# Output projection from scaled float16 pairs, gate sums from bfloat16 trees

## The chip, the cores and the metric

The kernel runs on one core of a Trainium2 chip. A core has TensorE (PE in the profile, with its weight loads as PEld), VectorE (DVE), ScalarE (ACT), GpSimd (POOL) and SyncE (SP, which only issues DMAs). Each engine takes its instructions in the order in which the program gives them. The metric is device time in microseconds of one execution; a lower time is better.

## The reference

One layer of a bidirectional encoder over 1024 tokens of width 1024, in float32. All inputs of the two attention groups come from one projection, and all outputs go through one more:

```python
h = jnp.einsum('bsd,de->bse', x, w_in[layer])
q_a, k_a, v_a, z_a, q_b, k_b, v_b, z_b = jnp.split(h, SPLIT_POINTS, axis=-1)
y_a = neighborhood_attention(...)          # 8 heads, windows of 8 x 16 on a 16 x 64 grid, learned bias
y_b = windowed_gqa_with_sink(...)          # 8 heads on 2 key heads, |i - j| <= 128, rotary, sink logit
mixed = jnp.concatenate([y_a * jax.nn.silu(z_a), y_b * jax.nn.silu(z_b)], axis=-1)
y = jnp.einsum('bse,ed->bsd', mixed, w_out[layer])
x = layer_norm(DEEPNORM_ALPHA * x + y, ln_gain[layer], ln_bias[layer])
```

The change concerns the last matrix product, `mixed @ w_out`: `mixed` has 1024 rows and 1024 columns, `w_out` is 1024 by 1024, and ALPHA is the fourth root of 2.

## The kernel before, in words

**Precision by pairs.** A float32 operand is split into a high part in a shorter type and a low part that holds the rest, and a product is three matmuls: high by high, high by low, low by high. The input projections (`project`, L355) use float16 pairs, for which x and the weights are first brought to a known magnitude by powers of two. The output projection (`out_mms`, L899) uses float32r pairs of `mixed` (tiles `m`, in `mh` and `ml`) and of `w_out` (tiles `wo`, in `wo_parts`), without a scale.

**Stages.** First V is projected (L430), while x is loaded and split. Then comes a prologue of six projections of 48 matmuls each (`ORDER[:6]`: zb0, z0, zb1, kb, qb0, z1). A program count runs along with these 288 matmuls: `run_to` emits one matmul, adds one to `ran`, and then runs what `at(c, ...)` has put at that count. So `at(219, w_scale, NPRO)` stands in every engine's order where the 219th matmul stands in PE's. After the prologue come 128 units of attention, one per step: scores on PE (`stage_qk`, L709 and L710) into one of four banks of PSUM with tag "s", bias and row minimum on DVE (L719), exponential on ACT (`stage_exp`, L735), high part on ACT (L745), low part on DVE (L746, which is the last reader of the bank), a DMA transpose, and six to nine steps later the product with V (`stage_pv`, L774), normalisation and transposition (L783, L794). The output of a head pair is multiplied into its gate tile (`stage_ot`, L797 and L803), which then holds the columns of `mixed`.

**Fill.** Between the units PE works off the other fifteen projections and the first 60 matmuls of the output projection (`out_head`), in portions that `FILL_AT` fixes by step. Each projection writes into one of two banks with tag "pj". A bank is free again when its last reader is done; for the gate z1 these are a tanh on ACT (L318) and a multiply on DVE (L319).

**Order.** The prologue and the units are in the order of the program text. In the units, ACT, DVE, POOL and SP also have software queues: `enq` puts an operation in, `pop` emits one or two ready ones per step, lower `prio` first and older first among equals, and `need` emits what must come now. Only `final`, the last phase, is ordered by the scheduler of the framework, from the dependences and its own estimates of times. It splits the last four head pairs and weight tiles 8 to 15, does the remaining 348 matmuls of the output projection, adds the residual (L946), and normalises rows.

**Weight scales.** `w_scan` (L201) and `sum_w` (L595 on ACT, L597 on DVE) form row sums of absolute weights; `w_scale` adds them over the partitions by a matmul with ones (L207), reduces the result on DVE (L208) and rounds it to a power of two (L209 to L212). `v_scale` and `x_scale` do the like for V and x.

**Tiles of the output weights.** `wo_load` loads them as `WO_LD` gives the steps, `wo_split` splits them (high part L860 on ACT or DVE, low part L864 on DVE or POOL) at the steps of `WO_AT` or in `final`.

Of the kernel before, what the change touches and what calls it, by code (L numbers as in the profile page):

```python
# [15 lines left out]
S = 1024  # L16
# [15 lines left out]
NS = 21 - NPRO  # L32
NR = 8
# [9 lines left out]
M_AT = [105, 112, 118, 120]  # L43
WO_AT = [67, 71, 75, 79, 128, 129, 130, 131]
# [11 lines left out]
def hybrid_block(ctx, tc, xT, x, wt, wv, wo, bias, sink, gain, lbias, cos, sin, bmask, out):  # L56
# [52 lines left out]
    sg = const.tile([128, 3], F32, name="sg")  # L109
    rsg = const.tile([128, 1], F32, name="rsg")  # L110
# [88 lines left out]

    def w_scan(m):  # L200
        nc.scalar.activation(junk[:, :512], raws[m].rearrange("p k c -> p (k c)"), AF.Abs, accum_out=wm[:, m:m + 1])  # L201

    def w_scale(n):
# [3 lines left out]
        nc.tensor.matmul(ps[:, :m], ones, wm.bitcast(BF16)[:, 2 * c + 1:2 * (c + m):2], start=True, stop=True)  # L207
        nc.vector.tensor_reduce(g, ps[:, :m], axis=mybir.AxisListType.X, op=ALU.add if n < NPRO else ALU.max)  # L208
        nc.vector.tensor_scalar_max(g, g, 2.0 ** -30)  # L209
        nc.vector.tensor_scalar(g.bitcast(I32), g.bitcast(I32), 0x7F800000, None, op0=ALU.bitwise_and)  # L210
        nc.vector.tensor_scalar(wsc[:, n:n + 1].bitcast(I32), g.bitcast(I32), 0x7F800000, None, op0=ALU.bitwise_xor)
        nc.vector.tensor_scalar(v, g, xrs, 0.5, op0=ALU.mult, op1=ALU.mult)  # L212
# [111 lines left out]
    def z_col(e):  # L324
        return vsc if e in (4, 0, 5) else vscb[:, 0:1] if e == 1 else vscb[:, 1:2]
# [8 lines left out]
    def project(name):  # L334
        n = ORDER.index(name)
        w_split(2 * n + 2)
        for half in range(2):
            ps = new_group()
            for k in range(KT):
# [9 lines left out]
                if n + 2 < NPRO and half == 1 and k == 6:  # L349
                    w_scale(n + 2)  # L350
# [27 lines left out]


    ordered = ExitStack()  # L380
    with ExitStack() as vctx:
# [69 lines left out]
        def x_scale():  # L451
            ps = bank("t")
            nc.tensor.transpose(ps[:, :128], gm.to_broadcast([128, 128]), identf)
            nc.vector.tensor_reduce(gm, ps[:, :128], axis=AXX, op=ALU.max)
            nc.vector.tensor_scalar_max(gm, gm, 2.0 ** -16)
            nc.vector.tensor_scalar(gm.bitcast(I32), gm.bitcast(I32), 0x7F800000, None, op0=ALU.bitwise_and)
            nc.vector.tensor_scalar_mul(xrs, gm, 2.0 ** -14)
            nc.vector.reciprocal(xsc, xrs)
# [69 lines left out]
        for i in range(8):  # L528
# [6 lines left out]
            for k in range(KT):  # L535
                v_mms(ps, 4 + i // 2, i % 2, k)
                if i == 1 and k == 2:
                    x_scale()
                if i in (2, 3) and k == 4:
                    w_scale(i - 2)  # L540
# [12 lines left out]
        vg = vw.tile([128, 1], F32, name="vg")  # L553

        def v_scale():
# [4 lines left out]
            nc.vector.tensor_scalar_max(vg, vg, 2.0 ** -100)  # L560
            nc.vector.tensor_scalar(vg.bitcast(I32), vg.bitcast(I32), 0x7F800000, None, op0=ALU.bitwise_and)
            nc.vector.tensor_scalar_mul(vsc, vg, 2.0 ** -14)
# [25 lines left out]

        def sum_w(i):
# [4 lines left out]
            if i not in (1, 4, 7):  # L594
                nc.scalar.activation(junk[:, :1024], t, AF.Abs, accum_out=wm[:, c:c + 1])  # L595
            else:
                nc.vector.tensor_reduce(wm[:, c:c + 1], t, axis=AXX, op=ALU.add, apply_absolute_value=True)  # L597
# [4 lines left out]

        at(16, v_scale)
        for t in range(9):
# [3 lines left out]
        for i in range(NS):  # L608
            at(14 + 14 * i, sum_w, i)
# [211 lines left out]
    EO = (4, 5, 6, 7, 0, 1, 2, 3)  # L821

    def m_alloc(e, pool):
        for parts_ in (mh, ml):
            if pool is big:
                parts_[e] = big_tile(f"m{e}", (128, S))
            else:
                parts_[e] = pool.tile([128, S], F32R, tag="m", name=f"m{e}", bufs=8)

    def m_split(e, sl, hi, lo):  # L830
        hi(mh[e][:, sl], zt[e][:, sl])
        lo(ml[e][:, sl], zt[e][:, sl], mh[e][:, sl].bitcast(F32))

    WO_SEQ = [(e, a) for a in range(2) for e in EO[:4]] + [(e, a) for e in EO[4:] for a in range(2)]
    wo_parts = {}

    wo_raw = {}
# [12 lines left out]
    def wo_split(n):  # L850
        def hi():
            if n < 8:
                t = big_tile(f"wo{n}")
            elif n < 13:
                t = tiles["fp"].tile([128, 2, 512], F32R, tag="wo", name=f"wo{n}", bufs=5)
            else:
                t = zp.tile([128, 2, 512], F32R, tag=("zc", "zd", "ze")[n - 13], name=f"wo{n}", bufs=1)
            wo_parts[n] = [t[:, 0, :], t[:, 1, :]]
            copy = nc.scalar.copy if hi_eng == "act" else nc.vector.tensor_copy
            copy(wo_parts[n][0], wo_raw[n])  # L860

        def lo():
            h, l = wo_parts[n]
            eng.tensor_sub(l, wo_raw.pop(n), h.bitcast(F32))  # L864

        eng, q = (nc.vector, "dve") if n % 3 == 2 else (nc.gpsimd, "pool")
        hi_eng = "act" if clock["step"] is not None or WO_SEQ[n][1] == 1 else "dve"
        o = enq(hi_eng, hi, load_ops.get(("wo", n)))
# [7 lines left out]
    def m_queue(e):  # L876
        m_alloc(e, big)
        m_ops[e] = []
        for h in (slice(0, 512), slice(512, S)):
            o = enq("act", lambda h=h: nc.scalar.copy(mh[e][:, h], zt[e][:, h]))  # L880
            m_ops[e].append(enq("pool", lambda h=h: nc.gpsimd.tensor_sub(
                ml[e][:, h], zt[e][:, h], mh[e][:, h].bitcast(F32)), o))
# [33 lines left out]
    def final():  # L916
# [13 lines left out]
        gb, bb = gain_tile[0], zslot("bb")  # L930
        nc.sync.dma_start(bb, lbias.partition_broadcast(128))
# [7 lines left out]
        def residual(t, a, ps, c=None):  # L939
            if a == 0:  # L940
                stats[t] = fp.tile([128, 4, 6], F32, tag="stats", name="stats")
            for k in range(2) if t == 7 and c is None else (c,):
# [3 lines left out]
                nc.vector.scalar_tensor_tensor(xv, xv, ALPHA, ps[:, o:o + w], op0=ALU.mult, op1=ALU.add)  # L946
                nc.vector.bn_stats(stats[t][:, a if k is None else 2 * a + k, :], xv)

        def row_stats(t):
# [3 lines left out]
            nc.scalar.activation(sd, mv[:, 1:2], AF.Sqrt, bias=eps)  # L953
# [83 lines left out]
    clock["step"] = 0  # L1037
    for i in range(-LD, NU + LO):
# [9 lines left out]
        for n in range(len(WO_LD)):  # L1048
            if WO_LD[n] == i:
                load_ops["wo", n] = enq("sp", lambda n=n: wo_load(n), wo_ops.get({9: 0, 10: 1, 12: 2, 13: 3}.get(n)),  # L1050
                                        w_ops.get(17 + n if 4 <= n <= 8 else None))
        for n in range(len(WO_AT)):
# [26 lines left out]
        if 0 <= i - LT < NU:  # L1079
            stage_tr(units[i - LT])  # L1080
        pump_to(i + F1)
# [90 lines left out]
```

## Time and profile before

| | us |
|---|---|
| median of three runs (455.21 to 455.54) | 455.3 |
| the profiled execution's own time | 455.19 |
| its span, first to last instruction | 453.4 |
| PE busy | 443.6 |
| DVE busy | 333.3 |
| ACT busy | 287.7 |
| POOL busy | 227.7 |

The granted TensorE clock was 0.995 on average. The phases by the trace: V until 61.9 us, the prologue until 124.1, the units until about 368, and the rest of the output projection until 445.7; what follows is the last tile's normalisation and store. In a row of the timeline stand the start, the length, the engine, the line, the operation, the tile written and the tiles read, the count of merged instructions, and in brackets the idle time ahead of it with what ended it. A row of groups has busy time and mean ns of one behind the bar. Lengths of matmuls overlap in the records; the distance between starts is what one costs.

### The profile page before, as it was taken

The page shows a single profiled execution, that of the slowest core. Times are in us where ns is not written, and L with a number is a line of the kernel's source. Part 1 is how long each engine was busy: PE and PEld are TensorE (multiplying, and loading weights), DVE is VectorE, ACT ScalarE, POOL GpSimd, SP SyncE. Part 2 cuts the span into 40 slices and gives each one's busy share as a digit, 9 for nine tenths or more (in the row PEclk, how much of TensorE's full clock was granted, in tenths as well). Part 3 has the DMA queues.
Part 4 walks back from the last instruction along what each step waited for, and adds up shares of the span by engine and source line. Part 5 has one row for each costly group of instructions (what it writes and reads, how often), then busy time and mean ns, then how long its engine had stood idle before and what let it go on. Part 6 is the DMA issues. An engine that isn't in the chain of part 4 may idle for free.

```text
span 453.4 us, 9438 instructions
## 1 busy us (share of the span) xinstructions
PE 443.6 (98%) x3260; PEld 295.2 (65%) x3260; DVE 333.3 (73%) x808; ACT 287.7 (63%) x664; POOL 227.7 (50%) x235
## 2 busy tenths in 40 slices
PE   8999999999999999999999999999999999999993
PEld 8999964444445565555555656555556788888882
DVE  5796956538987877896888878877878739099644
ACT  5648659776499877788777887686878825012100
POOL 0003944546848559688326766444773344007621
PEclk9999999999999999999999999999999999999998
DMA  8897277984657798599777989999999886004511
GB/s 263 275 328 259 78 256 248 322 307 167 209 114 150 157 174 158 113 140 170 162 170 159 167 173 214 195 147 200 218 189 234 159 249 267 1 19 147 187 55 57
DMA packets 134415, 82.28 MB, mean 181 GB/s; under 512 B 101344, under 2 KB 113504, under 8 KB 134112
## 3 DMA queue, kind: packets, MB, share of 16 engines
q1 hardware_dynamic: 133936, 81.26, 73.3%
q8 instruction: 25, 0.41, 0.4%
q10 hardware_dynamic: 432, 0.43, 0.4%
q14 instruction: 22, 0.18, 0.1%
HBM read 51.25 MB, written 9.96 MB: 135 GB/s over the span
## 4 chain that ended last, share of the span: by engine, by line
PE 88%; DVE 3%; issue 2%; POOL 2%; DMA 2%; ACT 2%; DVEq 0%; SPq 0%; POOLq 0%; ACTq 0%
PE ps_pj L355 42%; PE ps_s L899 9%; PE ps_s L430 6%; PE ps_t L774 6%; PE ps_pj L899 6%; PE ps_t L899 5%; PE ps_s L709 3%; PE ps_s L710 3%; PE ps_pj L430 3%; PE ps_t L430 3%; DMA bias<-in_bias 1%; PE ps_t L794 1%; DVE qs L240 1%; POOL ks L272 1%; ACT split L745 1%
## 5 line engine op out<-in xcount | busy, mean ns | idle before, releaser
L355 PE MATMUL ps_pj<-xf,wh 128*128 128x512 f16 x672 | 202.1, 379 | 0.9 <-DVE qs L240 0.6
L355 PE MATMUL ps_pj<-xf,wl 128*128 128x512 f16 x336 | 127.3, 379 | 0.0
L355 PEld LDWEIGHTS <-wh 128*128 128x128 f16 x672 | 63.5, 98 | 61.6 <-DVE ks L240 1.0
L735 ACT ACTIVATE ps_s<-sn,nm 128x385 f32<-128x385 f32 (+3 forms) x128 | 70.2, 549 | 33.0 <-DVE nm L719 31.8
L746 DVE SCALAR_TENSOR_TENSOR split<-ps_s,split 128x384 f16<-128x384 f32 (+2 forms) x128 | 65.6, 513 | 27.5 <-ACT split L745 26.0
L745 ACT ACTIVATE split<-ps_s 128x384 f16<-128x384 f32 (+2 forms) x128 | 57.4, 449 | 1.8
L355 PEld LDWEIGHTS <-wl 128*128 128x128 f16 x336 | 32.9, 98 | 37.4
L719 DVE CUSTOM_DVE_ANT_0 sn<-ps_s,bm,nsk 128x384 f32<-128x384 f32 (+1 forms) x64 | 40.8, 637 | 7.0 <-PE ps_s L710 6.4
L899 PE MATMUL ps_s<-wo,m 128*128 128x512 f32 (+1 forms) x192 | 43.3, 379 | 0.0
L719 DVE CUSTOM_DVE_ANT_0 sn<-ps_s,bias,sg 128x264 f32<-128x264 f32 (+1 forms) x64 | 35.0, 548 | 10.9 <-PE ps_s L710 3.1
L186 POOL TENSOR_SCALAR wr<-wr,wsc 128x512 f32<-128x512 f32 x26 | 20.6, 792 | 39.9 <-ACT wh L181 33.8
L709 PE MATMUL ps_s<-ks,qs 128*128 128x384 f16 (+4 forms) x128 | 39.3, 307 | 0.0
L710 PE MATMUL ps_s<-ks,qs 128*128 128x384 f16 (+4 forms) x128 | 39.2, 306 | 0.0
L681 POOL TENSOR_SCALAR bias<-bias,rsg 128x552 f32<-128x552 f32 (+1 forms) x24 | 19.2, 799 | 39.4 <-DMA bias<-in_bias 25.5
L899 PEld LDWEIGHTS ps_s<-wo,m 128*128 128x128 f32 x192 | 34.4, 188 | 7.0
L774 PEld LDWEIGHTS <-tr 128*128 128x128 f16 (+1 forms) x1104 | 36.5, 98 | 2.2 <-issue 0.3
L953 ACT ACTIVATE sd<-mv,eps 128x1 f32<-128x1 f32 x8 | 2.4, 294 | 49.9 <-DVE mv L951 45.8
L187 POOL TENSOR_TENSOR wl<-wr,wh 128x512 f16<-128x512 f32 x26 | 32.6, 1254 | 2.2
L272 POOL COPY ks<-ks 64x512 f16<-64x512 f16 x40 | 26.3, 665 | 10.3 <-DVE ks L240 5.4
L989 POOL TENSOR_TENSOR xr<-xr,gb 128x512 f32<-128x512 f32 x7 | 10.3, 1476 | 40.8 <-ACT xr L986 40.8
L430 PE MATMUL ps_s<-wvh,x 128*128 128x320 f32 x128 | 29.6, 311 | 0.0
L899 PE MATMUL ps_pj<-wo,m 128*128 128x512 f32 (+1 forms) x120 | 28.6, 376 | 0.0
(147 smaller groups left out, 827.4 us busy)
## 6 DMA issues: line engine op xcount, KB each, us to landing
xraw<-in_xT SPq DMA_DIRECT2D x31, 256.0 KB, 4.2
ws<-in_wt SPq DMA_DIRECT2D x15, 512.0 KB, 5.5
wr<-in_wt SPq DMA_DIRECT2D x26, 256.0 KB, 3.1
bias<-in_bias SPq DMA_DIRECT2D x16, 276.0 KB, 3.3
wor<-in_wo SPq DMA_DIRECT2D x16, 256.0 KB, 3.6
xr<-in_x SPq DMA_DIRECT2D x8, 512.0 KB, 6.7
out<-xr SPq DMA_DIRECT2D x14, 256.0 KB, 2.1
bias<-in_bias SPq DMA_DIRECT2D x8, 368.0 KB, 4.0
```

The lines of the kernel that those rows point to most:

```text
L187: nc.gpsimd.tensor_sub(l, raw, h)
L272: nc.gpsimd.tensor_copy(t[o, sl], t[a, sl])
L355: nc.tensor.matmul(ps, a[:, k % 4, :], mv, start=(k == 0 and i == 0), stop=(k == KT - 1 and i == 2))
L430: nc.tensor.matmul(ps[:, :320], lh[t // 4, k][:, ts], rh[k][:, cs], start=(k == 0 and i == 0), stop=(k == KT - 1 and i == 2))
L709: nc.tensor.matmul(ps[:, :m], q, sl[0], start=True, stop=False)
L710: nc.tensor.matmul(ps[:, :m], q, sl[1], start=False, stop=True)
L719: nc.vector.tensor_tensor_reduce(sn[:, :m], ps[:, :m], bias_t, sg[:, c:c + 1], init, op0=ALU.add, op1=ALU.min, accum_out=nm)
L735: nc.scalar.activation(pt[:, :m], sn[:, :m], AF.Exp, bias=nm, scale=-1.0, accum_out=sm[:, k:k + 1])
L745: nc.scalar.activation(hl[:, :m, 0, :c], src, AF.Copy, scale=PSCALE)
L746: nc.vector.scalar_tensor_tensor(hl[:, :m, 1, :c], src, PSCALE, hl[:, :m, 0, :c], op0=ALU.mult, op1=ALU.subtract)
L774: nc.tensor.matmul(ps[:, HD * m:HD * m + HD], a, b_, start=(i == 0), stop=(i == len(mms) - 1))
L899: nc.tensor.matmul(ps, lh[:, ts], rh[:, cs], start=(e == EO[0] and i == 0), stop=(e == EO[-1] and i == 2))
```

## The change

- **Output projection.** `m` and `wo` become float16 pairs. `m_alloc` keeps high and low of a head pair in one tile. A weight tile is multiplied by a power of two `wos` while it is split: the high part always on ACT, as an activation with a scale; the low part on DVE as one scalar_tensor_tensor, or on POOL as a multiplication followed by a subtraction. The gate columns carry a scale `msc` so that `mixed` stays inside float16's range; `z_col` returns `zcol`, the old factor times `msc`. The residual becomes ps times `oinv` plus x, where `oinv` undoes both scales and divides by ALPHA; the square root takes ALPHA squared as scale, and the gain is multiplied by ALPHA.
- **Bound of the gates.** `msc` needs a bound per gate column. For the eight gates ScalarE writes the absolute weights out in bfloat16 (`junk`, by halves), `z_tree` adds them on DVE in three adds down to 128 columns (`cs`), PE sums over the partitions (in `w_scale` for the prologue's gates, in `z_sum` for the others), and DVE takes the maximum (`z_max`). `m_scale`, at count 256, makes `zg`, `msc` and `zcol` of it in 13 instructions on 1 to 4 columns. The sum of zb2's weights moves from DVE to ACT, those of q3 and z3 trade places, and the prologue's `w_scale` comes at k = 7 instead of 6.
- **Scale of the output weights.** `wo_scan` takes the row sums of absolute values of each of the 16 weight tiles. Six tiles are loaded once more in the prologue and scanned there (counts 231 to 281); the other ten are scanned among the units after their load. At step 53 `need` emits what scans are left and `wo_max` reduces them; `wo_turn` transposes at step 62 and `wo_scale` does the rest in steps 63 to 65.
- **Memory.** Nine constant tiles and a 2 KB scrap tile are new, weight tiles 0 to 7 share four big tiles, and the reserve for DMA descriptors is 1024 bytes a partition.

The diff, cut to its core:

```diff
+ZPRO = (0, 1, 2, 5)
+ZSUM = (1, 5, 11, 14)
+DSUM = (4, 7)
+WO_PRE = (9, 10, 12, 13, 14, 15)
+WO_MAX = 53
...
+    def z_tree(n):
+        if n in zabs:
+            a = z_abs(n).rearrange("p (k c) -> p k c", c=128)
+            nc.vector.tensor_add(a[:, 0:4], a[:, 0:4], a[:, 4:8])
+            nc.vector.tensor_add(a[:, 0:2], a[:, 0:2], a[:, 2:4])
+            nc.vector.tensor_add(cs[:, zabs[n] % 4], a[:, 0], a[:, 1])
...
+        if n in ZPRO:
+            m = 128
+            nc.tensor.matmul(ps[:, :m], ones, cs[:, zabs[n] % 4], start=True, stop=True)
...
-                if n + 2 < NPRO and half == 1 and k == 6:
+                if n + 2 < NPRO and half == 1 and k == 3:
+                    z_tree(n + 2)
+                if n + 2 < NPRO and half == 1 and k == 7:
                     w_scale(n + 2)
...
+    def wo_scan(n):
+        nc.scalar.activation(scrap[:, :512], wo_raw[n], AF.Abs, accum_out=wom[:, n:n + 1])
...
-            if i not in (1, 4, 7):
-                nc.scalar.activation(junk[:, :1024], t, AF.Abs, accum_out=wm[:, c:c + 1])
+            if i in DSUM:
+                nc.vector.tensor_reduce(wm[:, c:c + 1], t, axis=AXX, op=ALU.add, apply_absolute_value=True)
+            elif i in ZSUM:
+                n = NPRO + i
+                zabs[n] = len(zabs)
+                nc.scalar.activation(z_abs(n), t, AF.Abs, accum_out=wm[:, c:c + 1])
+                for d, fn in ((23, z_tree), (47, z_sum), (51, z_max)):
+                    at(ran[0] + d, fn, n)
...
+        def m_scale():
+            nc.vector.tensor_reduce(zg, zc, axis=AXX, op=ALU.max)
+            for n in ZPRO:
+                nc.vector.tensor_max(zg, zg, wg[:, n:n + 1])
+            nc.vector.tensor_scalar_max(zg, zg, 2.0 ** -30)
+            nc.vector.tensor_mul(zg, zg, gm)
+            nc.vector.tensor_mul(zg, zg, vg)
+            nc.vector.tensor_scalar_mul(zg, zg, 2.0 ** 13 / 60000.0)
+            nc.vector.reciprocal(msc, zg)
+            for i, t in enumerate((vsc, vscb[:, 0:1], vscb[:, 1:2])):
+                nc.vector.tensor_mul(zcol[:, i:i + 1], t, msc)
...
+        at(256, m_scale)
+        for i in range(3):
+            at(200, wo_pre_load, i)
+        for i in range(len(WO_PRE)):
+            at(231 + 10 * i, wo_pre, i)
...
-            copy = nc.scalar.copy if hi_eng == "act" else nc.vector.tensor_copy
-            copy(wo_parts[n][0], wo_raw[n])
+            nc.scalar.activation(wo_parts[n][0], wo_raw[n], AF.Copy, scale=wos)
...
-            eng.tensor_sub(l, wo_raw.pop(n), h.bitcast(F32))
+            raw = wo_raw.pop(n)
+            if q == "dve":
+                nc.vector.scalar_tensor_tensor(l, raw, wos, h, op0=ALU.mult, op1=ALU.subtract)
+            else:
+                nc.gpsimd.tensor_scalar(raw, raw, wos, 1.0, op0=ALU.mult, op1=ALU.mult)
+                nc.gpsimd.tensor_sub(l, raw, h)
...
+        nc.scalar.mul(gb, gb, ALPHA)
...
-                nc.vector.scalar_tensor_tensor(xv, xv, ALPHA, ps[:, o:o + w], op0=ALU.mult, op1=ALU.add)
+                nc.vector.scalar_tensor_tensor(xv, ps[:, o:o + w], oinv, xv, op0=ALU.mult, op1=ALU.add)
...
-            nc.scalar.activation(sd, mv[:, 1:2], AF.Sqrt, bias=eps)
+            nc.scalar.activation(sd, mv[:, 1:2], AF.Sqrt, bias=eps, scale=ALPHA ** 2)
...
+                if n not in WO_PRE:
+                    scan_ops.append(enq("act", lambda n=n: wo_scan(n), load_ops["wo", n]))
+        if i == WO_MAX:
+            need(*scan_ops)
+            wo_max()
...
+        if i == WO_MAX + 9:
+            wo_turn()
+        if WO_MAX + 10 <= i < WO_MAX + 13:
+            wo_scale(i - WO_MAX - 10)
```

122 lines of the change are left out of this document (88 added, 34 removed).

## The prediction

> **What bounds the kernel now.** I read the page's busy times first, then who PE waits for, then the chain that ended last.
>
> ```profile
> PE 443.6 (98%) x3260; PEld 295.2 (65%) x3260; DVE 333.3 (73%) x808; ACT 287.7 (63%) x664; POOL 227.7 (50%) x235
> ```
>
> TensorE is busy 98% of 453.4 us. Its waits:
>
> ```profile
> PE ps_pj L355 <- DVE qs L240: 0.6, 1, 0.6
> ```
>
> That is its longest wait after the start. So time falls by what its matmuls get shorter, and rises by what makes it wait. The chain (start, length, what) gives the pitch of the matmuls by operand type, and the place where the units begin:
>
> ```profile
> 71.05 10.38 PE ps_pj L355 x48
> ...
> 124.48 1.29 PE ps_pj L355 x6
> ...
> 401.33 5.53 PE ps_pj L899 x24
> ...
> 442.80 2.87 PE ps_pj L899 x24
> ```
>
> A float16 matmul of 512 columns (L355) goes by every 10.38/48 = 0.216 us; a float32r one of the output projection (L899) every 5.53/24 = 0.230, and one of 256 columns every 2.87/24 = 0.120.
>
> **The gain: float16 output projection.** The rows of the tile wo count its matmuls (192 + 120 + 96 = 408); by the groups with shapes kept apart 360 have 512 columns and 48 (two tiles of 24) have 256:
>
> ```profile
> L899 PE MATMUL ps_s<-wo,m x192: 277/389/475, 359.4 to 442.5; 128*128 128x512 f32 x168, 128*128 128x256 f32 x24
> L899 PE MATMUL ps_pj<-wo,m x120: 276/389/525, 350.9 to 445.4; 128*128 128x512 f32 x96, 128*128 128x256 f32 x24
> L899 PE MATMUL ps_t<-wo,m x96: 387/391/477, 373.5 to 423.0; 128*128 128x512 f32 x96
> ```
>
> Two float16 products of 256 columns start 0.11 us apart:
>
> ```profile
> 224.25 0.27 PE L709 MATMUL ps_s<-ks,qs 128*128 128x256 f16 x1
> 224.36 0.27 PE L710 MATMUL ps_s<-ks,qs 128*128 128x256 f16 x1
> ```
>
> So 360 x 0.014 + 48 x 0.010 = 5.5 us, while PE stays the bound from 351 us on. At worst the 60 matmuls among the last units (x 0.014 = 0.8) and the start of the last phase gain nothing, and 4 us is left. The splits before that phase:
>
> ```profile
> 369.31 0.43 DVE L860 CAST wo<-wor 128x512 fp32r<-128x512 f32 x1 [5.06 <-DMA wor<-in_wo]
> 370.83 0.62 ACT L860 CAST wo<-wor 128x512 fp32r<-128x512 f32 x1 [7.55 <-DMA wor<-in_wo]
> ```
>
> Four high halves go from DVE (0.43) to ACT (0.62 each, 2.5 in all), and the gain vector's scaling adds one ACT pass, at most two such (1.3). ACT stands idle 7.55 us just there, since m of three finished head pairs and two weight tiles need no late DMA; that hides it. Without the cover it is up to 3.8 us at the phase's start. POOL's low half becomes two instructions (one more of 0.69, a row below); five of them against 7 us of POOL idle: nothing. The residual stays one DVE instruction; the square root only gets a constant. m's copies change type, not count. Three m and weight tiles share buffers that used to be separate: no new wait that I find. The smaller reserve for DMA descriptors and the new constant tiles move addresses and no work; z3's and q3's sums trade places at equal cost: nothing.
>
> **The price before the units: DVE.** The trees, sums and `m_scale` sit in the projections ahead of the units. Busy time of the engines there (PE, PEld, DVE, ACT, POOL):
>
> ```profile
> 82.00:103.00 21.00, 21.00 (x101) 9.56 (x100) 7.70 (x25) 14.55 (x28) 11.49 (x14) 1.00 0.95 318
> 103.00:124.00 21.00, 21.00 (x100) 9.52 (x99) 19.59 (x37) 11.93 (x20) 17.55 (x16) 1.00 0.52 184
> ```
>
> DVE has room up to 103 us and next to none after (19.59 of 21). The rows of DVE:
>
> ```profile
> 101.08 0.69 DVE L292 TENSOR_TENSOR rp_raw<-rp_raw,rp_sw 128x512 f32<-128x512 f32 x1
> 102.27 0.16 DVE L208 TENSOR_REDUCE wg<-ps_t 128x1 f32<-128x2 f32 x1 [0.50 <-PE ps_t L207]
> ...
> 104.19 0.01 DVE L289 LOAD_MASK_SELECT rp_sw<-rp_raw  x1 [0.77 <-ACT rp_raw L288]
> ...
> 112.81 0.15 DVE L209 TENSOR_SCALAR wg<-wg 128x1 f32<-128x1 f32 x1
> 112.99 0.15 DVE L210 TENSOR_SCALAR wg<-wg 128x1 int32<-128x1 int32 x1
> ...
> 114.25 0.70 DVE L292 TENSOR_TENSOR rp_raw<-rp_raw,rp_sw 128x512 f32<-128x512 f32 x1
> ...
> 120.32 2.63 DVE L242 TENSOR_TENSOR qs<-rp_raw,qs 64x512 f16<-64x512 f32 x2
> 122.98 0.69 DVE L319 SCALAR_TENSOR_TENSOR z<-z,ps_pj 128x512 f32<-128x512 f32 x1
> 123.70 1.53 DVE L242 TENSOR_TENSOR qs<-rp_raw,qs 64x512 f16<-64x512 f32 x2
> ...
> 125.92 0.53 DVE L719 CUSTOM_DVE_ANT_0 sn<-ps_s,bm,nsk 128x256 f32<-128x256 f32 x1
> ```
>
> From 104.19 on DVE runs without a pause. L319 at 122.98 frees, at 123.67, the bank into which PE's first projection among the units writes at 124.48: 0.81 us of slack. Program counts (one per matmul, 0.216 us; 288 is the end of the prologue) place the additions on this stretch:
> - A tree is three adds of 512, 256 and 128 bfloat16 values. No bfloat16 add is in the trace. Ends: float32 adds of 512 and 256 take 686 and 420 ns and a reduction of 128 291, 1.4 us together; a float16 copy of 256 takes 0.23, three of that kind 0.7. I take 1.0, between them, since the operands are 16 bits wide as the copy's but two are read.
>
> ```profile
> L401 DVE TENSOR_TENSOR x<-xraw,x 128x512 fp32r<-128x512 f32 x15 | 10.1, 686 | 1.6 <-ACT x L398 1.6
> ...
> L401 DVE TENSOR_TENSOR x<-xraw,x 128x256 fp32r<-128x256 f32 x2 | 0.8, 420 | 0.0
> ...
> L454 DVE TENSOR_REDUCE gm<-ps_t 128x1 f32<-128x128 f32 x1 | 0.3, 291 | 2.1 <-PE ps_t L453 2.1
> ```
>
> ```profile
> 72.79 0.23 DVE L572 COPY vb<-vt 128x256 f16<-128x256 f16 x1
> ```
>
> - Counts 177 to 191: z1's tree from 101.77 to 102.8, its scale (L208 to L217, 102.27 to 103.42 before, 0.13 more for the wider reduction, 0.2 for PE's sum) to 104.3, z2's tree to 105.3. DVE starts the full stretch 1.1 us late.
> - Count 219: a `z_max` (0.3) and z3's tree (1.0). Count 247: a `z_max` (0.3). Count 256: `m_scale`, 13 small instructions; dependent ones start 0.19 apart (112.81, 112.99): 2.4.
> - Together 1.1 + 0.3 + 1.0 + 0.3 + 2.4 = 5.1, less 0.81 of slack: PE waits 4.3 us for L319, and the first unit's L719 comes as late. On the way PE also waits about 2 us for z3's tree at count 243 (45 matmuls ahead of the units, so near 114.6 us; the tree ends near 117), which is inside the 4.3, since the same DVE queue sets the end. PE's own eight sums are 128 columns, 0.06 each by half of the 0.11 above: 0.2 lie before the stretch. Sum 4.5; ends 2.4 (short trees, small instructions closer together, less contention) and 7.2 (below).
> - What one tensor_tensor costs here depends on POOL: the L242 pair takes 2.63 us with POOL busy and 1.53 later, and POOL's own multiply 0.69 alone and 1.52 beside DVE:
>
> ```profile
> 63.03 0.69 POOL L186 TENSOR_SCALAR wr<-wr,wsc 128x512 f32<-128x512 f32 x1 [5.00 <-ACT wh L181]
> 118.23 1.52 POOL L186 TENSOR_SCALAR wr<-wr,wsc 128x512 f32<-128x512 f32 x1
> ```
>
> If each added two-input instruction waits so, z2's and z3's trees and `m_scale` take 2 to 3 us more.
>
> The earlier trees (zb0, z0, zb1, zb2, zb3) and the maxima there lie in DVE idle time; gone, each would cost its 1.0. The sum of zb2's weights moves from DVE to ACT, whose releases of the banks have a whole half projection (24 x 0.216 = 5.2 us) of room. The six early scans on ACT (under 0.85 each, rows below) lie between 111 and 124, where ACT is busy 11.93 of 21; their six loads go to SP, and the last waits for a scan that waits for DVE, with these loads queued behind it, which POOL holds anyway:
>
> ```profile
> 121.33 3.00 SPq L170 DMA_DIRECT2D wr<-in_wt  x2
> ```
>
> **The price among the units: ACT.** Ten more scans fall between steps 21 and 53 (155 to 222 us). The stretch's busy times, one scan of this kind, and who waits there:
>
> ```profile
> 155.00:222.00 67.00, 67.00 (x601) 38.51 (x599) 52.91 (x153) 53.05 (x135) 47.26 (x48) 1.00 0.83 151
> ```
>
> ```profile
> L201 ACT ACTIVATE junk<-wr 128x512 bf16<-128x512 f32 x12 | 7.6, 633 | 0.2
> ...
> L201 ACT ACTIVATION_READ_ACCUMULATOR junk<-wr 128x1 f32 x12 | 2.3, 194 | 0.0
> ```
>
> ```profile
> DVE split L746 <- ACT split L745: 9.3, 14, 1.3
> ACT ps_s L735 <- DVE nm L719: 9.2, 14, 1.2
> ...
> DVE sn L719 <- PE ps_s L710: 4.8, 7, 1.3
> ```
>
> A scan is 0.63 + 0.19 = 0.83 us, ten are 8.3. ACT is busy 53.05 of 67 us, so on average they fit (61.4). But ACT and DVE wait for each other in turn (9.3 and 9.2 us), and for PE only 4.8 us in all: that is what they can lose before PE notices. Ends: 0, when the scans fall into ACT's own 9.2 us of waiting, and 8.3 - 4.8 = 3.5. Behind a scan on ACT stands L745, and L746 on DVE waits for it. At step 53 the program emits what scans are left, and `wo_max` stands in DVE's queue ahead of the next L719, so DVE waits for them. I take 1.0, nearer to 0 because the average fits. DVE's `wo_scale` steps (six small instructions, 1.1 us) come in steps 63 to 65 against the same slack; `wo_turn` is 0.1 on PE. Splits of wo 0 to 7 in the loop: POOL 0.69 more for six of them, at 47.26 of 67 busy: nothing; were POOL full, 4 us.
>
> **Sum.** The profiled execution took 455.19 us (span 453.4, the rest around it), 0.11 under the median 455.3, to which I add: 455.3 - 5.5 + 4.5 + 1.0 + 0.1 = 455.4 us.
>
> **Two rules beside the rows.** The trace has 0.7 to 1.4 us for a tree. The Trainium skill, "VectorE: DVE Perf Modes", in "The perf-mode tier table", has tensor_tensor on bfloat16 in SBUF at twice the float32 rate; by the formula in its errata section, (N + 151)/0.96, with N halved, a tree is an estimated 0.94 us, and the sum would be 0.1 lower; by the float32 rows it would be 0.9 higher. No run here shows which. The second speaks against the change. The L242 pair varies between 1.53 and 2.63 us. The Trainium skill, "SBUF — State Buffer", in "Who interferes with whom", says that a VectorE instruction with two SBUF inputs and a GpSimd instruction that reads SBUF exclude each other, for the whole instruction. The pair's two times agree; what it would make of the sum is the second rival's.
>
> **Rivals.**
> 1. *Faster: the stretch before the units gives way.* Trees at 0.7, small instructions closer together, less contention for L242: 2.4 us, and the scans hide: 455.3 - 5.5 + 2.4 + 0.1 = 452.3. For it: the first L242 pair alone holds 1.1 us of contention (2.63 against 1.53). Against: DVE has no pause from 104.19 on. Chance 0.25.
> 2. *Slower: POOL holds the added two-input instructions up, from z2's tree on.* 7.2 instead of 4.5: 455.3 - 5.5 + 7.2 + 1.0 + 0.1 = 458.1. It decides from 4.4 us on. For it the pair at 120.32; against, POOL's work is limited, and a longer stretch lets it run dry. Chance 0.17.
> 3. *Slower: the scans fill ACT at steps 42 to 53* and PE waits 3.5: 457.9. Against: the average. Chance 0.08.
> 4. *The output projection does not get faster,* as its pitch hangs on other things than the type: 455.3 + 4.5 + 1.0 + 0.1 = 460.9. Against it L355's pitch with tiles of the same size. Chance 0.02.
>
> **Numbers.** The forecast, gain and waits nearly cancelling, has 0.48, with 454.0 to 457.0 as its own range. A measurement of this kernel can tell 0.2%, or 0.9 us, from no change. Of the 0.48, 0.33 lies within it, 0.12 above, 0.03 below. With the rivals: faster 0.28, same 0.33, slower 0.39. The range goes from rival 1 (452.3) past rival 2 to 458.6, since its waits and the scans' can add.
>
> **What will show it.** Right, if L899's pitch is 0.216; PE has a wait of about 4 us at the first projection among the units for L319, part of it at z3's sum; DVE has no pause from there back to 104 us; the steps 21 to 60 show PE waits of a us or so for L746's banks or for L719. Wrong in size, if the tree takes less than 0.7 or more than 1.4, or `m_scale` much other than 2.4. Wrong in kind, if PE's wait there is missing, or if the last phase begins with PE idle for a weight's half.

## The result: slower by 0.4 to 0.8%

The changed kernel took 458.56 us (median of six runs, 457.05 to 460.34) against 455.25 for the kernel before on the same chip: ratio 1.0075, 95% interval 1.005 to 1.010. On another chip, where it was run again as an experiment, the ratio was 1.0043, interval 1.0027 to 1.0058. The forecast of 455.4 was 2.3 to 3.2 us too low.

I read the profile after by its busy times first. The profiled execution took 458.96 us, its span is 457.2:

```profile
PE 440.8 (96%) x3265; PEld 263.2 (58%) x3265; DVE 346.8 (76%) x851; ACT 303.2 (66%) x703; POOL 234.4 (51%) x246
```

PE's busy time fell by 2.8 us while the span grew by 3.8, so PE now stands still. Its waits (for what; us in total, times, longest):

```profile
PE ps_t L640 <- DVE cs L233: 2.0, 1, 2.0
PE ps_pj L394 <- DVE qs L276: 1.9, 2, 1.4
PE ps_pj L394 <- DVE ks L276: 1.6, 1, 1.6
PE ps_t L434 <- DVE warm L431: 1.0, 1, 1.0
PE ps_pj L1009 <- POOL wo L975: 0.8, 1, 0.8
PE ps_s L801 <- DVE split L838: 0.5, 1, 0.5
PE ps_t L1009 <- POOL wo L975: 0.4, 1, 0.4
PE ps_pj L475 <- DVE x L443: 0.2, 1, 0.2
```

L434 and L475 are the start, which has such waits before too. The rest are three places. L640 is PE's column sum of z3's tree, ahead of the units. L394 and L801 are the projections and score products among the units; they wait for banks that VectorE frees (L276 is a low half of q or k, L838 that of the probabilities). L1009 is the output projection; it waits for GpSimd's low halves of the output weights.

To see how much each place cost, I took from the timeline when PE starts the score product of a given unit (the first is unit 0), and subtracted the kernel before. A row of each:

```profile
251.95 0.28 PE L709 MATMUL ps_s<-ks,qs 128*128 128x264 f16 x1
```

is unit 70 of the kernel before. Its other starts are 125.61 (unit 1), 173.10 (28) and 333.07 (112). The last column is the difference of the spans less that at unit 112.

| kernel | unit 1 | 28 | 70 | 112 | from 112 to the end | ratio to before (95%) |
|---|---|---|---|---|---|---|
| changed | +3.8 | +3.8 | +7.7 | +7.7 | -4.0 | 1.0075 (1.005 to 1.010) |
| changed, run again | +4.0 | +4.0 | +7.9 | +7.9 | -5.2 | 1.0043 (1.0027 to 1.0058) |
| 1 gain's factor in the constant | +3.7 | +3.7 | +7.6 | +7.6 | -5.7 | 1.0049 (1.0037 to 1.0061) |
| 2 no scans among the units | +3.7 | +3.7 | +4.4 | +4.4 | -5.7 | 0.9976 (0.9966 to 0.9985) |
| 3 z3's sum and m_scale later | +1.4 | +2.7 | +7.2 | +7.2 | -5.7 | 1.0032 (1.0017 to 1.0046) |
| 4 = 1, 2 and 3 | +0.8 | +2.1 | +3.3 | +3.3 | -5.7 | 0.9955 (0.9940 to 0.9970) |
| 5 projection alone | +0.2 | +0.2 | +0.2 | +0.2 | -5.9 | 0.9876 (0.9863 to 0.9890) |
| 6 z3's sum on PE, short m_scale | +0.9 | +0.9 | +4.9 | +4.9 | -5.7 | 1.0002 (0.9987 to 1.0017) |
| 7 wo_max late | +3.9 | +3.9 | +5.8 | +6.2 | -5.2 | 1.0024 (1.0013 to 1.0035) |
| 8 all kept, mended | +0.9 | +0.9 | +0.9 | +1.2 | -5.6 | 0.9911 (0.9897 to 0.9925) |
| 9 as 8, gain scaled on ScalarE | +1.7 | +1.7 | +1.7 | +2.0 | -5.6 | 0.9916 (0.9897 to 0.9935) |

So the changed kernel loses 3.8 us ahead of the units, nothing to unit 28, 3.9 between units 28 and 70, and wins 4.0 to 5.2 behind unit 112, where the kernels without a wait in the last phase win 5.6 to 5.9.

**The gain.** The chain of the changed kernel (start, length, what) has the new pitch:

```profile
407.69 5.18 PE ps_pj L1009 x24
...
446.57 2.63 PE ps_pj L1009 x24
```

5.18/24 = 0.216 us and 2.63/24 = 0.110, as forecast.

**Ahead of the units.** VectorE's timeline in the changed kernel (start, length): z1's tree, a row of `w_scale` (L245, L209 before), z3's tree, the second of the two maxima, m_scale from L667 to L676, and L355, which frees the first bank of the projections among the units:

```profile
101.47 0.42 DVE L231 TENSOR_TENSOR junk<-junk 128x512 bf16<-128x512 bf16 x1
101.93 0.29 DVE L232 TENSOR_TENSOR junk<-junk 128x256 bf16<-128x256 bf16 x1
102.25 0.23 DVE L233 TENSOR_TENSOR cs<-junk 128x128 bf16<-128x128 bf16 x1
...
112.98 0.15 DVE L245 TENSOR_SCALAR wg<-wg 128x1 f32<-128x1 f32 x1
...
114.73 0.79 DVE L231 TENSOR_TENSOR junk<-junk 128x512 bf16<-128x512 bf16 x1
115.56 0.58 DVE L232 TENSOR_TENSOR junk<-junk 128x256 bf16<-128x256 bf16 x1
116.17 0.23 DVE L233 TENSOR_TENSOR cs<-junk 128x128 bf16<-128x128 bf16 x1
121.54 0.28 DVE L644 TENSOR_REDUCE zc<-ps_t 128x1 f32<-128x128 f32 x1
124.31 0.16 DVE L667 TENSOR_REDUCE zg<-zc 128x1 f32<-128x4 f32 x1
124.50 1.39 DVE L669 TENSOR_TENSOR zg<-zg,wg 128x1 f32<-128x1 f32 x4
...
127.11 0.68 DVE L355 SCALAR_TENSOR_TENSOR z<-z,ps_pj 128x512 f32<-128x512 f32 x1
```

z1's tree took 1.01 us from its first start to its last end, z3's 1.67, and m_scale 2.80 (124.31 to 127.11). L355 comes 4.13 us later than L319 did (122.98).

**Among the units.** ACT and DVE around step 53, where the last two scans (L423) are forced and wo_max (L928) waits for them:

```profile
226.90 0.62 ACT L423 ACTIVATE scrap<-wor 128x512 bf16<-128x512 f32 x1
227.42 0.19 ACT L423 ACTIVATION_READ_ACCUMULATOR scrap<-wor 128x1 f32 x1
227.64 0.63 ACT L423 ACTIVATE scrap<-wor 128x512 bf16<-128x512 f32 x1
228.17 0.19 ACT L423 ACTIVATION_READ_ACCUMULATOR scrap<-wor 128x1 f32 x1
```

```profile
228.39 0.17 DVE L928 TENSOR_REDUCE wog<-wom 128x1 f32<-128x16 f32 x1 [1.41 <-ACT scrap L423]
```

**The last phase.** SP's, ACT's, POOL's and PE's rows of the timeline:

```profile
374.79 0.43 SPq L1146 DMA_DIRECT2D gb<-in_gain  x1
...
382.95 1.06 ACT L1041 ACTIVATE gb<-gb 128x1024 f32<-128x1024 f32 x1 [11.73 <-DMA gb<-in_gain]
...
385.85 0.69 POOL L974 TENSOR_SCALAR wor<-wor,wos 128x512 f32<-128x512 f32 x1 [10.23 <-ACT wo L966]
...
391.01 0.59 PE L1009 MATMUL ps_pj<-wo,m 128*128 128x512 f16 x2 [0.77 <-POOL wo L975]
```

The scaling of the gain vector stands first among ScalarE's instructions of the last phase, although the program writes it behind the splits. So ScalarE idles 11.73 us for the load, the high halves of the output weights stand behind it, GpSimd's low halves behind those (10.23 us idle), and PE waits.

### The profile page after: what moved, and what is told of

Its sections match the earlier page's. It is cut to its first block, busy times and chain, and to the rows that moved or that the text cites. A ratio compares the mean times of both kernels' runs of the same rounds, so it can differ in the third digit from the quotient of the medians.

```text
span 457.2 us, 9549 instructions
## 1 busy us (share of the span) xinstructions
PE 440.8 (96%) x3265; PEld 263.2 (58%) x3265; DVE 346.8 (76%) x851; ACT 303.2 (66%) x703; POOL 234.4 (51%) x246
## 4 chain that ended last, share of the span: by engine, by line
PE 67%; issue 9%; DVE 7%; POOL 7%; DMA 4%; ACT 4%; SPq 0%; DVEq 0%; POOLq 0%; ACTq 0%
PE ps_pj L394 30%; PE ps_s L475 6%; PE ps_s L1009 5%; PE ps_t L866 5%; PE ps_pj L1009 4%; PE ps_s L801 3%; PE ps_pj L475 3%; PE ps_s L802 3%; PE ps_t L475 3%; PE ps_t L1009 3%; POOL wl L202 3%; DMA xr<-in_x 2%; POOL wr L201 2%; DVE sn L811 1%; DMA wor<-in_wo 1%
## 5 line engine op out<-in xcount | busy, mean ns | idle before, releaser
L394 PE MATMUL ps_pj<-xf,wh 128*128 128x512 f16 x672 | 203.3, 381 | 3.6 <-DVE qs L276 1.9
L394 PE MATMUL ps_pj<-xf,wl 128*128 128x512 f16 x336 | 128.1, 381 | 0.0
L394 PEld LDWEIGHTS <-wh 128*128 128x128 f16 x672 | 63.8, 98 | 67.1 <-issue 5.8
L838 DVE SCALAR_TENSOR_TENSOR split<-ps_s,split 128x384 f16<-128x384 f32 (+2 forms) x128 | 65.6, 513 | 31.4 <-ACT split L837 30.2
L1009 PEld LDWEIGHTS <-m 128*128 128x128 f16 x408 | 39.6, 98 | 43.1 <-issue 2.3
L394 PEld LDWEIGHTS <-wl 128*128 128x128 f16 x336 | 33.0, 98 | 37.7 <-issue 0.6
L201 POOL TENSOR_SCALAR wr<-wr,wsc 128x512 f32<-128x512 f32 x26 | 21.8, 838 | 43.5 <-ACT wh L196 37.3
L1009 PE MATMUL ps_s<-wo,m 128*128 128x512 f16 (+1 forms) x192 | 40.8, 366 | 0.0
L801 PE MATMUL ps_s<-ks,qs 128*128 128x384 f16 (+4 forms) x128 | 39.2, 306 | 0.5 <-DVE split L838 0.5
L475 PE MATMUL ps_s<-wvh,x 128*128 128x320 f32 x128 | 29.4, 309 | 0.0
L1009 PE MATMUL ps_pj<-wo,m 128*128 128x512 f16 (+1 forms) x120 | 26.6, 358 | 0.8 <-POOL wo L975 0.8
L523 POOL TENSOR_SCALAR xraw<-xraw,xsc 128x512 f32<-128x512 f32 x5 | 4.5, 907 | 39.2 <-ACT xf L521 39.2
L827 ACT ACTIVATION_READ_ACCUMULATOR ps_s<-sn,nm 128x1 f32 x128 | 24.1, 188 | 0.0
```

The lines of the kernel that those rows point to most:

```text
L201: nc.gpsimd.tensor_scalar(raw, raw, scale, 1.0, op0=ALU.mult, op1=ALU.mult)
L394: nc.tensor.matmul(ps, a[:, k % 4, :], mv, start=(k == 0 and i == 0), stop=(k == KT - 1 and i == 2))
L475: nc.tensor.matmul(ps[:, :320], lh[t // 4, k][:, ts], rh[k][:, cs], start=(k == 0 and i == 0), stop=(k == KT - 1 and i == 2))
L801: nc.tensor.matmul(ps[:, :m], q, sl[0], start=True, stop=False)
L827: nc.scalar.activation(pt[:, :m], sn[:, :m], AF.Exp, bias=nm, scale=-1.0, accum_out=sm[:, k:k + 1])
L838: nc.vector.scalar_tensor_tensor(hl[:, :m, 1, :c], src, PSCALE, hl[:, :m, 0, :c], op0=ALU.mult, op1=ALU.subtract)
```

## The experiments

(The kernels of experiments 7 and 8 have the labels e8 and e7, those of experiment 9 e9 and e10.)

The theory after the result, called A: three separate losses, each in its own queue (VectorE ahead of the units; ScalarE's scans among the units; the gain vector at the head of ScalarE's queue in the last phase), against a gain of 5.5 us that arrived in full. The first four kernels take one loss away each, and all three.

### 1. The gain vector's factor in the square root's constant

```
-        nc.scalar.mul(gb, gb, ALPHA)
...
-        nc.vector.memset(eps, EPS)
+        nc.vector.memset(eps, EPS / ALPHA ** 2)
...
-            nc.scalar.activation(sd, mv[:, 1:2], AF.Sqrt, bias=eps, scale=ALPHA ** 2)
+            nc.scalar.activation(sd, mv[:, 1:2], AF.Sqrt, bias=eps)
```

> The scaling of the gain vector on ScalarE is left out, and its factor goes into the constant of the square root instead (EPS / ALPHA squared, no scale), so the output stays the same. Theory A (four separate terms; ScalarE's queue at the start of the last phase waits 11.7 us for the gain vector's load, and the halves behind it reach PE late): the PE waits of 0.9 and 0.6 us for the low halves at 390 and 397 us go, 1.5 us faster than the changed kernel, about 457. Rival (the halves are late because GpSimd's low half became two instructions): the same time within 0.3 us, and PE waits there as before.

457.51 us, ratio 1.0049. PE's waits in this kernel, in full:

```profile
PE ps_t L640 <- DVE cs L233: 2.0, 1, 2.0
PE ps_pj L394 <- DVE qs L276: 1.9, 2, 1.4
PE ps_pj L394 <- DVE ks L276: 1.6, 1, 1.6
PE ps_pj L394 <- DVE z L355: 1.2, 1, 1.2
PE ps_t L434 <- DVE warm L431: 1.0, 1, 1.0
PE ps_s L801 <- DVE split L838: 0.5, 1, 0.5
```

The waits at L1009 are gone, with GpSimd's two-instruction halves still there, so the rival falls. But by the times the size stays open: 1.0049 lies under the first 1.0075, with intervals that overlap, and is no better than the 1.0043 of the changed kernel run again (experiment 9). A wait for L355 has appeared, which the first profile did not have; see the hardware section.

### 2. No scans among the units

```
-                if n not in WO_PRE:
-                    scan_ops.append(enq("act", lambda n=n: wo_scan(n), load_ops["wo", n]))
...
+        nc.vector.memset(wom, 0.0)
```

> The ten scans of output weights among the units are left out; the scale comes from the six weights scanned ahead of the units (the other ten columns of maxima are zero), and nothing waits at step 53. Theory A: PE's idle time between 222 and 311 us falls from 4.2 us to the 0.5 of the kernel before, so 3.5 us faster than the changed kernel, about 455. Rival (the units stall because they begin 3.8 us late and the projections between them with them, not for the scans): PE still idles 3 to 4 us there, same time within 1 us.

454.2 us, ratio 0.9976. The units begin as late as in the changed kernel (+3.7 at unit 1) and lose only 0.65 us between units 28 and 70, where the changed kernel loses 3.9. So the scans and what follows from them cost 3.25 us, and the later start costs nothing there: the rival falls. The 0.65 left lies beside wo_scale's six small VectorE instructions of steps 63 to 65, which this kernel keeps.

### 3. z3's sum and m_scale later

```
-                for d, fn in ((23, z_tree), (47, z_sum), (51, z_max)):
+                for d, fn in ((23, z_tree), (75 if i == 14 else 47, z_sum), (81 if i == 14 else 51, z_max)):
...
-        at(256, m_scale)
...
+        if 4 <= i < 17:
+            next(m_steps, None)
```

> Trees stay where they are; PE's sum of z3's tree goes from 24 matmuls behind it to 52 behind it, its maximum from 28 to 58, and the thirteen small instructions of m_scale go one by one into steps 4 to 16 of the units. Theory A (PE stops at that sum because VectorE is late, and runs at half clock after the stop): no wait at the sum, granted clock 1.0 between 114 and 121 us, the first unit 3 to 3.8 us earlier, 455 in all. Rival 1 (VectorE's added work sets the end whatever PE waits for): the wait moves to the bank of the first projection among the units, less m_scale's 2.9 us, and half of the gain at most, 456.5. Rival 2 (the half clock comes by itself, not from the wait): the granted clock dips in the same place, 1.7 us of the gain are missing.

456.43 us, ratio 1.0032. The wait at the sum is gone. The first unit starts 3.1 us earlier than in the changed kernel (124.77 against 127.90), as theory A has it, and unit 1 2.4 us earlier; but by unit 28 half of that is lost again (+1.4 becomes +2.7), in the steps where m_scale's thirteen instructions now stand (two of them, L671 and L672, took 0.77 and 1.06 us there, 0.16 each in the changed kernel). By the time it lies at the first rival's 456.5: VectorE's added work costs nearly as much in the units' first steps as ahead of them. Rival 2 gets no support, as there was no dip of the clock; nor is it excluded, as experiment 1 has none either.

### 4. The three edits together

> The three edits together: gain vector's factor in the square root's constant, no scans among the units (scale from the six weights scanned earlier), z3's sum and m_scale later. Theory A, terms add: the loss of the change is gone but for 0.5 to 1 us, so 455.3 - 5.5 + 0.5 to 1 = 450.3 to 451. Rival (one shared cause, VectorE's and GpSimd's competition, so that what is won in one place is lost in the next): 453 or more.

453.12 us, ratio 0.9955: above the 450.3 to 451 of theory A, and at the rival's 453. The table has what is missing: +2.1 us at unit 28, from the work of experiment 3 moved instead of removed, and 1.1 more until unit 70. Whether that is work moved or one shared cause, this kernel alone can't tell; experiments 6 and 8 do.

### 5. The float16 projection alone

```
-ZPRO = (0, 1, 2, 5)
-ZSUM = (1, 5, 11, 14)
-DSUM = (4, 7)
+ZPRO = ()
+ZSUM = ()
+DSUM = (1, 4, 7)
...
-        at(256, m_scale)
...
+        nc.vector.memset(wos, 2.0 ** 14)
+        nc.vector.memset(msc, 2.0 ** 9)
+        nc.vector.memset(oinv, 2.0 ** -23 / ALPHA)
```

> The float16 output projection alone: the gates' and the output weights' scales are constants, so there are no trees, no column sums, no m_scale, no scan of output weights, no wo_max to wo_scale and no scaling of the gain vector (its factor in the square root's constant); the halves, their two-instruction form on GpSimd and their places are the change's. Theory A (the gain is 5.5 us as predicted and the losses are only in the three places): 455.4 - 5.5 = 449.9, between 449.5 and 450.5, PE's waits as in the kernel before. Rival (a fourth loss in the halves themselves, or a gain that is smaller, as some of the matmuls lie beside units): 451 or more, with PE waits behind 335 us.

449.6 us against 455.41, ratio 0.9876: by the ratio 5.65 us, 5.5 forecast. PE's waits are those of the kernel before:

```profile
PE ps_t L434 <- DVE warm L431: 1.0, 1, 1.0
PE ps_pj L394 <- DVE qs L276: 0.6, 1, 0.6
PE ps_pj L394 <- DVE ks L276: 0.4, 1, 0.4
```

So there is no fourth loss: the halves, their two instructions on GpSimd, and the splits among the units cost nothing, as forecast. All that is lost is what this kernel leaves out, the making of the scales and the gain vector's scaling: 9 us by the changed kernel's first ratio (1.0075 - 0.9876 = 0.0199 of 455.4), 7.6 by its second.

### 6. Less work for VectorE ahead of the units

```
+        def z_sum8(n):
+            zps[n] = bank("t")
+            for k in range(8):
+                nc.tensor.matmul(zps[n][:, :128], ones, z_abs(n)[:, 128 * k:128 * k + 128], start=k == 0, stop=k == 7)
...
         def m_scale():
...
+            nc.vector.tensor_reduce(zg, zc, axis=AXX, op=ALU.max)
+            nc.vector.tensor_scalar(zg, zg, gm, 2.0 ** -46, op0=ALU.mult, op1=ALU.max)
+            nc.vector.tensor_scalar(zg, zg, vg, 2.0 ** 13 / 60000.0, op0=ALU.mult, op1=ALU.mult)
+            nc.vector.reciprocal(msc, zg)
+            nc.vector.tensor_scalar_mul(zcol, vs3, msc)
```

(`zc` holds all eight maxima here, `vs3` the three factors side by side.)

> The changed kernel with less work on VectorE before the units: z3's tree is left to PE (eight matmuls of 128 columns into one bank, 7 more than before, about 0.4 us of PE), and m_scale does the same with five instructions in place of thirteen. Theory A (the length of VectorE's queue sets when the units begin; the tree took 1.6 us and m_scale 2.9, of which some 1.9 go): first unit 3 us earlier than the changed kernel's 127.9, so about 125, and 455.6 in all. Rival (GpSimd holds VectorE up in this stretch, so that fewer small instructions help little): first unit at 126.5 or later, 457 or more.

455.09 us, ratio 1.0002, 0.5 under theory A's 455.6. VectorE's timeline:

```profile
123.47 0.16 DVE L672 TENSOR_REDUCE zg<-zc 128x1 f32<-128x8 f32 x1
...
124.36 0.23 DVE L676 TENSOR_SCALAR zcol<-vs,msc 128x3 f32<-128x3 f32 x1
124.50 0.68 DVE L355 SCALAR_TENSOR_TENSOR z<-z,ps_pj 128x512 f32<-128x512 f32 x1
```

m_scale takes 1.03 us instead of 2.80, z3's tree is gone, and L355 comes 2.61 us earlier; the first unit starts at 124.42, inside theory A and far from the rival's 126.5, and unit 1 2.9 us earlier than in the changed kernel, at 126.52. The length of VectorE's queue sets it, where experiment 3 had only moved it.

### 7. wo_max late

```
-WO_MAX = 53
+WO_MAX = 84
-WO_AT = [67, 71, 75, 79, 128, 129, 130, 131]
+WO_AT = [97, 99, 101, 103, 128, 129, 130, 131]
```

> All ten scans stay among the units, but wo_max goes from step 53 to 84 (so that no scan is forced there), PE's transpose and the three steps of wo_scale follow at 93 to 96, and the splits of output weights 0 to 7 of the loop go from steps 67 to 79 to 97 to 103. Theory A (the ten scans' time on ScalarE, between units 29 and 56, uses up the 1 to 3 us that lie between a unit's split and its bank's next use): at most 1.5 us faster than the changed kernel, 457 or more, and PE still waits 2 us or more between 222 and 311. Rival B (the two forced scans at step 53, wo_max's wait for them and wo_scale's steps do it): 3 us or more faster, 455.5, PE's waits of that stretch under 1.

456.17 us, ratio 1.0024. Neither theory A nor its rival was right: between units 28 and 70 it loses 2.0 us, half of the changed kernel's 3.9 (and 0.4 more by unit 112, where wo_max and wo_scale now stand). PE's waits for the projections' banks (of the first row's two, one comes only at 340 us, where the kernel before waits 0.6 too):

```profile
PE ps_pj L394 <- DVE qs L276: 1.3, 2, 0.7
PE ps_pj L394 <- DVE ks L276: 1.1, 1, 1.1
```

So the scans cost 2.0 us even where none is forced, and the other 1.9 are the forcing of two of them at step 53, wo_max's wait and wo_scale's steps (beside which experiment 2 had 0.65 left); these three were moved together.

### 8. All that the change computes, mended

The edits of 1, 6 and 7, and the ten scans at fixed steps:

```
+SCAN_AT = (20, 24, 28, 68, 70, 72, 74, 76, 78, 80)
...
+        if i in SCAN_AT:
+            n = scans.pop(0)
+            scan_ops.append(enq("act", lambda n=n: wo_scan(n), load_ops["wo", n]))
```

The steps come from the kernel before: the time from the end of a unit's split (L746) to the score product four units on, which takes the same bank, is 3.0 to 4.5 us in units 18 to 28, 1.1 to 3.4 in units 32 to 65, and 2.1 to 4.8 in units 67 to 85. An enqueued scan runs some steps later: by ScalarE's timeline the ten ran behind the exponentials of units 22, 28, 30 and 72 to 83, in the changed kernel behind those of 22, 27, 30 and 36 to 52. So three hardly moved, and seven did.

> Nothing is left out: the gain vector's factor in the square root's constant, z3's sum by PE and m_scale in five instructions, wo_max at 84 as above, and the ten scans at fixed steps, 20, 24, 28 and seven from 68 to 80, where a unit's split ends 3 to 5 us ahead of its bank's next use. Theory A: PE's waits between 222 and 311 us as in the kernel before, first unit at about 125, no wait in the last phase: 455.4 - 5.5 + 1 to 2 = 451 to 452, faster than both kernels. Rival (scans cost wherever they stand, as ScalarE and VectorE wait for each other in turn): 454 or more.

451.05 us, ratio 0.9911, inside theory A's 451 to 452 and faster than both kernels. Between units 28 and 70 nothing is lost, and between 70 and 112, where the seven scans now are, 0.3, as in experiment 7, which has no scan there; so the scans cost nothing at these places, and the rival falls. What stays of PE's waits, but for 0.2 us at the start:

```profile
PE ps_t L435 <- DVE warm L432: 1.0, 1, 1.0
PE ps_pj L395 <- DVE qs L277: 0.7, 1, 0.7
PE ps_pj L395 <- DVE z L356: 0.4, 1, 0.4
PE ps_pj L395 <- DVE ks L277: 0.4, 1, 0.4
```

### 9. The changed kernel again, and 8 with the gain vector scaled

> The changed kernel once more, unedited, for a second profile and a time beside the next kernel's. Theory A (the wait for the gain vector is there in every execution, and PE feels it only where the load lands as late as the 8.1 us of the first profile; it took 6.5 to 6.9 us in three of the kernels that keep the scaling): ScalarE idles 9 to 12 us for the gain vector; PE waits behind 385 us for low halves of the output weights if the load takes 8 us, and not if it takes 6.5. The granted clock between 117 and 121 us may be 0.6 or 1.0, and the second unit starts at 129.3 to 129.5 either way. 457 to 459.

> The kernel in which all is kept and mended (451.05), but with the gain vector's scaling left on ScalarE as the change has it. Theory A: ScalarE idles 9 us or more for the gain vector ahead of the last phase's halves; PE waits there in some executions, so 0 to 1.5 us slower than 451.05, 451 to 452.6. Rival (the 1.2 us that the constant in the square root gained came from something else than that wait, such as one pass less on ScalarE): ScalarE's idle time there is under 8 us, or the time is as without it although PE waits.

The changed kernel took 457.69 us (1.0043), the other 451.71 (0.9916 against 0.9911: no difference that the intervals show; its +1.7 at unit 1 against +0.9 arises ahead of the wait at L355, which is as long and comes 0.8 us later). In the changed kernel's second profile, the same row and PE's waits:

```profile
381.92 1.06 ACT L1041 ACTIVATE gb<-gb 128x1024 f32<-128x1024 f32 x1 [10.52 <-DMA gb<-in_gain]
```

```profile
PE ps_pj L394 <- DVE z L355: 1.2, 1, 1.2
...
PE ps_t L1009 <- POOL wo L975: 0.4, 1, 0.4
```

ScalarE's idle time for the gain vector was 9.5 to 11.7 us in all profiles of kernels that scale it. By the DMA view the load took 8.1 us in the first profile (PE's gaps behind 385 us 1.64 in sum), 7.4 in the second (0.55), 6.8 in the last kernel (none), 6.5 in experiment 2 (none), and 6.7 in experiment 7 (0.42). So the load's own time does not order them, but its landing does, counted from PE's last score product: 17.2 us behind it in the first profile, 16.0 in the second, 15.9 in experiment 7, and 15.0 to 15.5 in the four kernels that scale the gain vector and have no such wait. The mechanism is shown, and that it is a matter of how late the load lands. Its mean price stays open: between 0 and 1.2 us by the two ratios of the changed kernel against experiment 1's.

## Why the prediction was wrong

- **The gain, 5.5.** Right: the pitches as forecast, 5.65 us alone.
- **VectorE ahead of the units, +4.5.** Right in place and mechanism, 3.8 at unit 1 (4.0 in the second profile). The parts erred both ways. The late start of 1.1 us had nearly vanished further down the queue (the row of L209 stood at 112.81, L245 stands at 112.98: 0.17), since instructions in between took less: the add of L291 1.64 us before and 1.09 as L327, the pair of L242 1.81 before and 1.40 as L278. z3's tree took 1.67 instead of 1.0, and m_scale 2.80 instead of 2.4, of which the four one-column maxima are 1.39 where spacing of 0.19 would have made 0.76. That PE's wait at z3's sum is no extra cost but part of one queue's length is shown by the second profile: 2.1 us there, 1.4 more at L355 (both as time between matmul starts beyond the pitch), together 3.5; PE came 0.5 us late to this stretch. In the first profile the wait at L355, whose absence the prediction called wrong in kind, is missing: PE lost 1.7 us to a lower clock there instead (last section).
- **Two rules.** The Trainium skill, "VectorE: DVE Perf Modes", by the formula in its errata section, gave an estimate of 0.94 us for a tree. z1's tree, with 1.01, agrees. The Trainium skill, "SBUF — State Buffer", in "Who interferes with whom", has a two-input VectorE instruction and GpSimd exclude each other; z3's adds (0.79 and 0.58 against z1's 0.42 and 0.29) fit it. No run here takes GpSimd's work away alone, so the cause of these 0.66 us is argued and not shown.
- **The scans among the units, +1.0.** This is the step that failed. The sentence was "I take 1.0, nearer to 0 because the average fits". With wo_max and its wait they cost 3.25 to 3.9 us, close to or past the upper end of 3.5. The average over 67 us did fit (ACT was busy 56.57 of 67 with eight of the ten scans in that stretch, first row below), and PE was at 67.00 there; the loss came behind it. The last two rows are the kernel before.

```profile
155.00:222.00 67.00, 67.00 (x598) 38.17 (x596) 50.43 (x149) 56.57 (x149) 45.61 (x46) 1.00 0.79 146
222.00:245.00 23.00, 21.10 (x194) 12.23 (x193) 18.58 (x49) 17.56 (x46) 6.37 (x8) 1.00 0.72 159
245.00:260.00 15.00, 13.39 (x128) 7.83 (x127) 12.94 (x40) 11.67 (x31) 8.68 (x13) 1.00 0.96 170
...
222.00:245.00 23.00, 22.65 (x202) 12.84 (x201) 19.79 (x54) 16.86 (x45) 7.93 (x11) 1.00 0.77 169
245.00:260.00 15.00, 15.00 (x141) 9.01 (x139) 13.01 (x35) 12.74 (x34) 10.15 (x14) 1.00 0.90 173
```

  (Stretch, length, then busy time of PE, PEld, DVE, ACT, POOL.) PE lost 1.90 of 23 us and 1.61 of 15 right behind the stretch that I had averaged, 0.35 and nothing before. What fell ahead of the loss is the reserve from unit to unit (as in experiment 8), 1.9 to 3.4 us at units 42 to 54 before. Each scan takes up to 0.8 of it, and it fell to 0.05 at units 45 and 52 in the changed kernel (in experiment 7, which forces none, at unit 45 alone). The waits that followed were mostly for the low halves of q and k (L276), which come behind the units' work on VectorE, and only 0.5 us for L838; the prediction named L746's banks and L719. So the reserve tells how far VectorE and ScalarE have fallen behind PE, and is not itself the bank that PE mostly waits for. The prediction's 9 us of waits of ACT and DVE for each other were no room for the scans: in the same steps (158.8 to 225.8 us here) ACT still waits 9.2 us for DVE, and DVE waits 12.2 for ACT instead of 9.3. Nor were DVE's 4.8 us of waiting for PE what can be lost before PE notices: 3.8 of them are still there. Rival 3 named the mechanism with 457.9, at a chance of 0.08.
- **The start of the last phase, nothing.** Wrong in kind, as its last paragraph allowed: "ACT stands idle 7.55 us just there, ... that hides it". The idle time was there, but the instruction that I laid into it waits for a DMA of 6.5 to 8.1 us and stood ahead of the splits. Cost 0 to 1.6 us in the profiles.
- **GpSimd's second instruction, the splits among the units: nothing.** Right by experiment 5. That kernel has no wo_turn and no wo_scale; the stretch where they stand lost 0.65 us in experiment 2 and 0.3 in experiment 8, against the 0.1 of the sum.

The sum with what was measured: 455.3 - 5.65 + 3.8 + 3.9 + 0 to 1.6 = 457.4 to 459.0; the two medians were 458.6 and 457.7.

## What to carry to other kernels

Price work on a helper engine by the reserve at the unit where it lands (end of the last reader of a bank to its next writer), not by the engine's busy share of a long stretch: the ten scans, unforced, cost 2.0 us with seven of them at units 36 to 55, and nothing with these seven at units 72 to 83. Where VectorE's queue was full, removing instructions paid (experiment 6), while moving them behind the next start gave back half of what it won (experiment 3). An instruction that needs a late load belongs at the end of its queue, or its factor into a constant that some other instruction reads anyway.

## What the runs showed of the hardware

After PE's wait at L640 (2.1 us between matmul starts beyond the pitch) the granted clock of the first profile fell to about half for a while; in the second profile of the same kernel it didn't. The stretch 117 to 121 us (length, PE, PEld, DVE, ACT, POOL, then the granted clock) of the first profile, and of the second:

```profile
117.00:121.00 4.00, 4.00 (x13) 1.51 (x12) 3.86 (x8) 2.57 (x5) 3.19 (x3) 0.60 0.98 335
```

```profile
117.00:121.00 4.00, 4.00 (x20) 1.82 (x20) 3.90 (x7) 2.57 (x5) 2.73 (x3) 1.00 1.02 334
```

Eight matmuls went at 0.427 us each, 1.7 us more than at 0.216. Of the five profiles with this wait three have it (the first, experiments 2 and 7), two have not (experiment 1, the second). It cost next to nothing: where it came, L355's bank was free before PE got there (0.33 us before in the first profile), and unit 1 started at 129.33 to 129.46; where it did not, PE waited 1.4 us for L355 and unit 1 started at 129.31 and 129.58. The Trainium skill, "TensorE: Matmul & The Clock Gate", in "What's actually happening", has the half rate after an idle window of about 3.4 us; here it came after a wait of 2.1, in three of five. The half rate's length, 8 x 0.427 = 3.4 us, fits that window. What decides whether it comes is open.
